# A gated output projection in a hybrid decoder block: the gate row in the weights, parked weights back by transfers, x on other queues

## The chip, the core and the metric

The kernel runs on one core of a Trainium2 chip. The metric is the device time of one execution in microseconds (us). The engines named below are PE (TensorE, matmuls), DVE (VectorE), ACT (ScalarE), POOL (GpSimd) and SP (SyncE, which here only issues transfers). Each engine works through its own list of instructions in order, and waits on semaphores for the others; a transfer (DMA) is issued by SP or ACT from that same list, so whatever waits in front of it holds it back.

## The reference, cut to what matters

Everything is float32; the sequence has 1024 rows and the model 1024 columns, the FFN 2816.

```python
mod = silu(c) @ w_ada + b_ada
sh1, sc1, g1, sh2, sc2, g2 = split(mod, 6)
h = rms_norm(x, norm_mix_g) * (1 + sc1) + sh1
proj = h @ w_in + b_in
...
y = (g_conv * y_conv + g_mlstm * y_mlstm) @ w_out
x = x + g1 * y
h = rms_norm(x, norm_ffn_g) * (1 + sc2) + sh2
gt, up = split(h @ w_ffn_up, 2)
x = x + g2 * ((silu(gt) * up) @ w_ffn_down)
return rms_norm(x, final_norm_g)
```

`g1` and `g2` are rows of 1024 values, the same for all rows of the sequence.

## The kernel before

Matmuls are done in three products per block: each float32 operand is split into a high part (a copy by ACT) and a low part (a subtraction by DVE), and PE adds high x high, low x high and high x low.

The stretch that the change touches lies in the middle of the kernel:

- **The end of the merge.** For eight column blocks `e`, PE multiplies the convolution's output by `w_conv_pw` (L158). DVE adds the bias and the gate (L926), adds the other mixer's part (L927), ACT writes the high part of `y` (L930), DVE the low part (L931). In the background DVE builds the four rows `g1`, `sh2`, `sc2`, `g2` of `mod` from 32 pieces of `w_ada` (`awt`, L900), PE transposes the sums (L904), and the result stands as columns in `modc`.
- **The gate rows.** After the last of these, PE transposes the columns of `g1` and `g2` (L939), ACT copies them (L940), SP stores them to a small array in HBM (`mrow_d`, L942). SP then loads the row of `g1`, repeated over 128 partitions, into `g1row` (L945); the row of `g2` is loaded later.
- **The output projection**, `w_out_part`: two halves `q` of the sequence times two halves `eh` of the columns, so four parts. Each has four chunks `kk` of `w_out`, 512 KB each: SP loads one into one of two buffers `wraw` (L996), ACT writes `whi` (L997), DVE writes `wlo` (L998), two buffers each. PE does 24 matmuls of 128 x 512 per chunk (L1003 to L1005) into four banks. At a part's end DVE multiplies each bank by `g1row` (L1009) and adds it to `x` (L1010), and ACT squares it for the norm (L1011). After the second `eh`, SP stores the new rows (`x1_d`, L1013) and they are scaled by their norm (L1016, L1018).
- **Beside it**: ACT issues the loads of `x` (L986). Two blocks of up weights (`f` = 0 and 1) are loaded early (L1047), combined (L1060 to L1065), split and *parked* in those halves of the tiles `Th` and `Tl` that are still free (`up_park`); later `up_unpark` copies them on ACT into the tiles `u` and `s` (L1097), which take the place of `y`. `h2_parts` transposes the normalized rows (L1028) and builds the seven-product operands of the up projection (`Bh`, `Th`, `Dh` and their low parts), which starts right after the projection (`up_run`, L1114 to L1116).

A scheduler sets the order on each engine from the order of the code and its priorities; `queue_behind` pins one instruction behind another on the same engine, and the table `AT` says at which of the 68 steps of the projection a task of the side work is put in. Tiles of a pool share space with tiles of earlier pools, and a load into one waits until the old tile's readers are done.

Of the kernel before, what the change touches and what calls it, by code (L numbers as in the profile page):

```python
# [8 lines left out]
F32 = mybir.dt.float32  # L9
# [8 lines left out]
KT = 8  # L18
NH = 4
FF = 2816  # L20
# [28 lines left out]
def hybrid_block(ctx: ExitStack, tc: tile.TileContext, x, c, w_ada, b_ada, norm_mix_g, w_in, b_in,  # L49
# [832 lines left out]

    modc = const.tile([128, 4, KT], F32, name="modc")

    def ada_task(ch, half):
# [24 lines left out]
        for k2 in range(4):  # L910
            bg.append((1300, lambda k2=k2: step(k2)))
# [19 lines left out]
            nc.vector.tensor_sub(y_lo, sg[:, q * 512:(q + 1) * 512], y_hi.bitcast(F32))  # L931
    pump(10 ** 9)
    credit[0] = 0.0
    g1, sh2, sc2, g2 = (modc[:, i, :] for i in range(4))
    mrow_d = [dram.tile([8, 128], F32, name=f"mrow_d{i}") for i in range(2)]
    p = ps_a()
    mrow = ap_.tile([8, 2, 128], F32, name="mrow", tag="act", bufs=3)
    for i, t in enumerate((g1, g2)):
        nc.tensor.transpose(p[0:8, i * 128:(i + 1) * 128], t, ident)  # L939
    nc.scalar.activation(mrow, p[0:8, 0:256].rearrange("p (i d) -> p i d", i=2), AF.Copy)  # L940
    for i in range(2):
        nc.sync.dma_start(mrow_d[i], mrow[:, i])  # L942

    def mod_row(i, t):
        nc.sync.dma_start(t, mrow_d[i].rearrange("(o k) d -> o (k d)", o=1).to_broadcast([128, D]))  # L945

# [21 lines left out]
    def krow(name):  # L968
        return up_.tile([128, D], F32, name=name, tag="krow", bufs=1)

    Bh = [big.tile([128, 2, 512], F32R, name=f"Bh{k}", tag="xa") for k in range(4)]
    Bl = [big.tile([128, 2, 512], F32R, name=f"Bl{k}", tag="xa") for k in range(4)]
    Th = [tp.tile([128, 4, 512], F32R, name=f"Th{k}") for k in range(4)]
# [7 lines left out]
        rsqrt(y, v)  # L981
        return y

    def load_x(t, xs):
        x = kx("x1")
        nc.scalar.dma_start(x, x2[t * 128:(t + 1) * 128, :])  # L986
        xs.append(x)

    evicted = {}

    def w_out_part(q, eh, xs, ss, banks):
        es = slice(eh * 512, (eh + 1) * 512)
        for kk in range(4):
            raw, hi, lo = (wp.tile([128, KT, 128], dt, name=n, tag=n).rearrange("p (k a) e -> p k (a e)", a=4)
                           for n, dt in (("wraw", F32), ("whi", F32R), ("wlo", F32R)))
            nc.sync.dma_start(raw, wo[kk * 256:(kk + 1) * 256, es].rearrange("(k p) e -> p k e", p=128))  # L996
            nc.scalar.activation(hi, raw, AF.Copy)  # L997
            nc.vector.tensor_sub(lo, raw, hi.bitcast(F32))  # L998
            y_hi, y_lo = (yt[q][j][kk] for j in range(2))
            for t in range(4):  # L1000
                ts_ = slice(t * 128, (t + 1) * 128)
                for k in range(2):
                    nc.tensor.matmul(banks[t], y_hi[:, k, ts_], hi[:, k, :], start=(kk == 0 and k == 0), stop=False)  # L1003
                    nc.tensor.matmul(banks[t], y_lo[:, k, ts_], hi[:, k, :], start=False, stop=False)
                    nc.tensor.matmul(banks[t], y_hi[:, k, ts_], lo[:, k, :], start=False, stop=(kk == 3 and k == 1))  # L1005
                yield
        for t in range(4):
            x = xs[t][:, es]
            nc.vector.tensor_mul(banks[t], banks[t], g1row[:, es])  # L1009
            evicted["v"] = nc.vector.tensor_add(x, x, banks[t])  # L1010
            evicted["s"] = nc.scalar.activation(banks[t], x, AF.Square, scale=1.0 / 32, accum_out=ss[:, t, eh:eh + 1])  # L1011
            if eh == 1:
                nc.sync.dma_start(x1_d[4 * q + t], xs[t])  # L1013
# [29 lines left out]
    def weights(kind, name):  # L1043
        return wp.tile([128, KT, 128], F32 if kind == "wraw" else F32R, name=name, tag=kind)

    def up_load(f, t, col0):
        nc.sync.dma_start(t, wup[:, col0 + f * 128:col0 + (f + 1) * 128].rearrange("(k p) e -> p k e", p=128))  # L1047
        return t

    def split_into(hi, lo, t):  # L1050
# [2 lines left out]
        return hi, lo  # L1053

    def up_sums(f, gate=True, behind=None):
        g = up_load(f, weights("wraw", "graw") if gate else k4("graw").rearrange("p (k e) -> p k e", k=KT), 0)
        u = up_load(f, k4("uraw").rearrange("p (k e) -> p k e", k=KT), FF)
# [32 lines left out]
    def up_unpark(f, s3):  # L1090
# [3 lines left out]
        for kp, name in ((3 - 2 * f, "u"), (2 - 2 * f, "s")):  # L1094
            pair = xb_pair(name)
            for t, src in zip(pair, spare(kp)):
                nc.scalar.activation(t.rearrange("p (a b) e -> p a (b e)", b=2), src.bitcast(F32), AF.Copy)  # L1097
            w.append(pair)
        return w + [s3]

# [79 lines left out]
        nc.vector.tensor_sub(lo, raw, hi.bitcast(F32))  # L1180
        return hi, lo

    xs0, xs1 = [], []
# [153 lines left out]
```

## Time and profile before

| what | value |
|---|---|
| three runs | 1732.58, 1734.45 (median), 1735.91 us |
| the profiled execution | 1735.88 us |
| its span, first to last instruction | 1734.1 us |
| granted clock of PE, mean over the span | 0.996 |

A row of a list of instructions has the start in us, the duration, the engine, the line, the operation and its tiles (out<-in), how many rows are merged, and in brackets how long the engine was idle before it and what ended that. "SPq" or "ACTq" in the engine's place are instructions that the engine only issues. A row of the waits says who waited for what: the total in us, how often, the longest. A row of windows has a stretch of the span, its length, the busy time of each engine with the number of instructions, the granted clock, the DMA engines' busy share and GB/s. A row of a line's summary has the number of instructions and the shortest, median and longest duration in ns.

### The profile page before, as it was taken

The numbers are of one execution on the slowest core, as the hardware profiler recorded it, in microseconds if no ns is written. First come the engines' busy times: TensorE is split into PE (matmuls) and PEld (weight loads), VectorE is DVE, ScalarE is ACT, GpSimd is POOL, SyncE is SP. The second block draws the span as 40 slices with busy tenths as digits, with TensorE's granted clock in tenths as the row PEclk, the third lists the DMA queues.
The fourth block names the chain that finished last, engine by engine and source line by source line (L and its number), as shares of the span: only waits on it lengthen the run. The fifth ranks groups of instructions, "written<-read, shape, count | busy, mean of one in ns | idle before, by whom it ended". The sixth has DMA issues, their size and how long they took to land. (4 is left out here: it accounts for less than half of the span.)

```text
span 1734.1 us, 20875 instructions
## 1 busy us (share of the span) xinstructions
PE 1692.9 (98%) x8360; PEld 1418.6 (82%) x8360; DVE 1249.7 (72%) x1681; ACT 611.7 (35%) x809; POOL 52.7 (3%) x113
## 2 busy tenths in 40 slices
PE   5999999999999999999999998999999999999998
PEld 4788889888988888888888778888888888778887
DVE  6989998997799669446798668766666665685243
ACT  7424335323433253223522386322222222232122
POOL 0000001000001000000000000000000000000000
PEclk9999999999999999999999999999999999999999
DMA  9221120221111112243694743322222222653121
GB/s 320 63 62 49 37 71 28 61 73 49 37 49 61 61 49 61 73 146 98 209 376 167 230 152 104 98 86 85 86 73 75 84 81 96 226 168 101 58 94 52
DMA packets 194711, 179.91 MB, mean 104 GB/s; under 512 B 7463, under 2 KB 166711, under 8 KB 194615
## 3 DMA queue, kind: packets, MB, share of 16 engines
q1 hardware_dynamic: 177367, 146.61, 27.4%
q10 hardware_dynamic: 17248, 31.99, 5.0%
q8 instruction: 65, 1.06, 0.3%
q14 instruction: 31, 0.25, 0.0%
HBM read 146.06 MB, written 32.51 MB: 103 GB/s over the span
## 5 line engine op out<-in xcount | busy, mean ns | idle before, releaser
L388 DVE SCALAR_TENSOR_TENSOR cacc<-a,col,cacc 128x1024 f32<-128x1024 f32 x240 | 306.8, 1286 | 3.9 <-ACT cacc L386 1.4
L158 PE MATMUL mm<-hh,wlo 128*128 128x512 f32 x864 | 271.2, 391 | 1.5 <-DVE wlo L149 1.5
L158 PE MATMUL mm<-hl,whi 128*128 128x512 f32 x864 | 272.5, 392 | 0.0
L158 PE MATMUL mm<-hh,whi 128*128 128x512 f32 x864 | 271.6, 392 | 0.0
L158 PEld LDWEIGHTS mm<-hh,wlo 128*128 128x128 f32 x864 | 160.3, 188 | 33.6 <-DVE wlo L149 2.7
L158 PEld LDWEIGHTS mm<-hl,whi 128*128 128x128 f32 x864 | 161.0, 188 | 32.1 <-issue 0.5
L158 PEld LDWEIGHTS mm<-hh,whi 128*128 128x128 f32 x864 | 160.5, 188 | 31.6
L148 ACT ACTIVATE whi<-wraw 128x1024 fp32r<-128x1024 f32 x61 | 64.7, 1061 | 226.5 <-PE mm L158 171.3
L149 DVE TENSOR_TENSOR wlo<-wraw,whi 128x1024 fp32r<-128x1024 f32 x61 | 74.5, 1222 | 28.7 <-ACT whi L148 25.2
L1114 PE MATMUL mm<-Bh,gh 128*128 128x512 f32 (+1 forms) x192 | 71.5, 375 | 2.9 <-ACT gh L1051 1.5
L1115 PE MATMUL mm<-Bl,gh 128*128 128x512 f32 (+1 forms) x192 | 71.5, 373 | 0.6 <-DVE Bl L1033 0.6
L604 PE MATMUL mm<-wlo,hh 128*128 128x256 f32 x256 | 72.0, 282 | 0.0
L1116 PE MATMUL mm<-Bh,gl 128*128 128x512 f32 (+1 forms) x192 | 71.2, 371 | 0.0
L1303 DVE TENSOR_TENSOR x<-x,mm 128x1024 f32<-128x1024 f32 x24 | 29.3, 1219 | 52.0 <-PE mm L1301 49.6
L1179 ACT ACTIVATE whi<-wraw 128x512 fp32r<-128x512 f32 (+2 forms) x32 | 25.3, 792 | 114.8 <-PE mm L1301 75.8
L535 DVE SCALAR_TENSOR_TENSOR cacc<-qkraw,col,cacc 128x1024 f32<-128x1024 f32 x48 | 61.5, 1282 | 4.9 <-ACT cacc L533 4.5
L603 PE MATMUL mm<-whi,hh 128*128 128x256 f32 x192 | 54.6, 284 | 0.0
L605 PE MATMUL mm<-whi,hl 128*128 128x256 f32 x192 | 54.2, 283 | 0.0
L1299 PE MATMUL mm<-fa,whi 128*128 128x512 f32 x128 | 50.6, 396 | 1.6 <-DVE cu L1142 0.9
L1300 PE MATMUL mm<-fa,wlo 128*128 128x512 f32 x128 | 50.5, 395 | 1.2 <-DVE wlo L1180 1.2
L1301 PE MATMUL mm<-fa,whi 128*128 128x512 f32 x128 | 50.6, 395 | 0.0
L1052 DVE TENSOR_TENSOR ul<-uraw,uh 128x1024 fp32r<-128x1024 f32 x20 | 24.5, 1225 | 35.4 <-ACT uh L1051 35.4
(444 smaller groups left out, 3893.1 us busy)
## 6 DMA issues: line engine op xcount, KB each, us to landing
wraw<-in_w_in_dram SPq DMA_DIRECT2D x64, 512.0 KB
awt<-in_w_ada_dram SPq DMA_DIRECT2D x32, 512.0 KB
graw<-in_w_ffn_up_dram SPq DMA_DIRECT2D x24, 512.0 KB
uraw<-in_w_ffn_up_dram SPq DMA_DIRECT2D x22, 512.0 KB
draw<-in_w_ffn_down_dram SPq DMA_DIRECT2D x22, 512.0 KB
act_d<-cg ACTq DMA_DIRECT2D x38, 256.0 KB
wad<-in_w_ada_dram SPq DMA_DIRECT2D x16, 512.0 KB
wraw<-in_w_out_dram SPq DMA_DIRECT2D x16, 512.0 KB
```

Source lines behind the costliest of these rows:

```text
L148: nc.scalar.activation(hi, raw, AF.Copy)
L149: (eng or nc.vector).tensor_sub(lo, raw, hi.bitcast(F32))
L158: nc.tensor.matmul(flat(acc)[:, a:b], lhs[:, k, :], rhs[k][:, a:b], start=(first and k == 0), stop=(last and k == kt - 1))
L388: nc.vector.scalar_tensor_tensor(acc, a[:, j:j + S], dw_col(j, ct), acc, op0=OP.mult, op1=OP.add)
L535: nc.vector.scalar_tensor_tensor(cv, raw[:, j:j + S], wcol(j), cv, op0=OP.mult, op1=OP.add)
L603: nc.tensor.matmul(o, hh[k][:, ts_], his[k], start=False, stop=False)
L604: nc.tensor.matmul(o[:, 0:256], hh[k][:, ts_], los[k], start=False, stop=False)
L605: nc.tensor.matmul(o, hl[k][:, ts_], his[k], start=False, stop=(k == KT - 1))
L1114: nc.tensor.matmul(o, a, rh, start=(k == 0), stop=False)
L1115: nc.tensor.matmul(o, a, rl, start=False, stop=False)
L1116: nc.tensor.matmul(o, b, rh, start=False, stop=(k == 3))
L1299: nc.tensor.matmul(o, hi[:, i, :], his[i][:, a:b], start=(i == 0), stop=False)
```

## The change

Four things are changed.

1. The row of `g1` is stored as soon as its columns are done (`store_row`, inside the background task of `mod`), the row of `g2` likewise at the end; the load of `g1row` is issued ahead of the projection, and so are the loads of the first `x` rows.
2. In `w_out_part`, each loaded chunk of `w_out` is multiplied by the row (L1006) before it is split; the multiply of each bank at a part's end is gone. What is computed is `y @ (w_out * g1)`.
3. `up_unpark` moves the parked blocks by eight transfers on SP's queue (L1108) in the place of eight copies on ACT.
4. The stores of `x1_d` are issued by ACT (L1022) in the place of SP; the two parked blocks' loads are pinned behind the last w_out load issued so far.

```diff
+    def store_row(ch):
+        p = ps_a()
+        mrow = ap_.tile([8, 128], F32, name="mrow", tag="mrow", bufs=1)
+        nc.tensor.transpose(p[0:8, 0:128], modc[:, ch, :], ident)
+        nc.scalar.activation(mrow, p[0:8, 0:128], AF.Copy)
+        nc.sync.dma_start(mrow_d[ch // 3], mrow)
...
+                if half and ch in (0, 3):
+                    store_row(ch)
...
-    p = ps_a()
-    mrow = ap_.tile([8, 2, 128], F32, name="mrow", tag="act", bufs=3)
-    for i, t in enumerate((g1, g2)):
-        nc.tensor.transpose(p[0:8, i * 128:(i + 1) * 128], t, ident)
-    nc.scalar.activation(mrow, p[0:8, 0:256].rearrange("p (i d) -> p i d", i=2), AF.Copy)
-    for i in range(2):
-        nc.sync.dma_start(mrow_d[i], mrow[:, i])
...
+    g1row = krow("g1row")
+    mod_row(0, g1row)
...
+    for t in range(4):
+        load_x(t, xs0)
...
-            nc.sync.dma_start(raw, wo[kk * 256:(kk + 1) * 256, es].rearrange("(k p) e -> p k e", p=128))
+            evicted["q"] = nc.sync.dma_start(raw, wo[kk * 256:(kk + 1) * 256, es].rearrange("(k p) e -> p k e", p=128))
+            nc.vector.tensor_mul(raw, raw, g1row[:, None, es].to_broadcast([128, 2, 512]))
...
-            nc.vector.tensor_mul(banks[t], banks[t], g1row[:, es])
             evicted["v"] = nc.vector.tensor_add(x, x, banks[t])
...
-                nc.sync.dma_start(x1_d[4 * q + t], xs[t])
+                nc.scalar.dma_start(x1_d[4 * q + t], xs[t])
...
-    def up_load(f, t, col0):
-        nc.sync.dma_start(t, wup[:, col0 + f * 128:col0 + (f + 1) * 128].rearrange("(k p) e -> p k e", p=128))
+    def up_load(f, t, col0, behind=None):
+        ins = nc.sync.dma_start(t, wup[:, col0 + f * 128:col0 + (f + 1) * 128].rearrange("(k p) e -> p k e", p=128))
+        if behind:
+            queue_behind(ins, behind["q"])
         return t
...
-                nc.scalar.activation(t.rearrange("p (a b) e -> p a (b e)", b=2), src.bitcast(F32), AF.Copy)
+                nc.sync.dma_start(t.rearrange("p (a b) e -> p a (b e)", b=2).bitcast(F32), src.bitcast(F32))
...
-    g1row = krow("g1row")
-    mod_row(0, g1row)
...
-    for t in range(4):
-        load_x(t, xs0)
```

The change moves instructions on three engines. First DVE, where the merge ends and the projection begins. Numbers tell buffers apart; the last two blocks of the merge are `t4b_7392` and `t4b_7481` before and the last is `t4b_7493` in the change; the first chunk of w_out is `wraw_7621` before and `wraw_7624` in the change. Before, around the last two blocks:

```order
L926 SCALAR_TENSOR_TENSOR t4b_7392<-mm_7402,col2_528,t4b_7392 128x1024
L998 TENSOR_TENSOR wlo_7623<-wraw_7621,whi_7622 128x1024
L900 SCALAR_TENSOR_TENSOR aacc_7451<-awt_7464,sc_c_102,aacc_7451 128x512
L906 TENSOR_REDUCE modc_6817<-pa_7379 128x4
L927 TENSOR_TENSOR t4b_7392<-t4b_7392,t4b_7393 128x1024
```
```order
L926 SCALAR_TENSOR_TENSOR t4b_7481<-mm_7491,col2_528,t4b_7481 128x1024
L998 TENSOR_TENSOR wlo_7653<-wraw_7651,whi_7652 128x1024
L908 TENSOR_TENSOR modc_6817<-modc_6817,col6_117 128x4
L927 TENSOR_TENSOR t4b_7481<-t4b_7481,t4b_7482 128x1024
L931 TENSOR_TENSOR y013_6825<-t4b_7481,y003_6821 128x512
L931 TENSOR_TENSOR y113_6833<-t4b_7481,y103_6829 128x512
L998 TENSOR_TENSOR wlo_7683<-wraw_7681,whi_7682 128x1024
```

And in the change (L937, L938 and L942 are the former L926, L927 and L931; L1006 is the new multiply, L1008 the former L998):

```order
L937 SCALAR_TENSOR_TENSOR t4b_7493<-mm_7503,col2_528,t4b_7493 128x1024
L938 TENSOR_TENSOR t4b_7493<-t4b_7493,t4b_7494 128x1024
L942 TENSOR_TENSOR y013_6827<-t4b_7493,y003_6823 128x512
L942 TENSOR_TENSOR y113_6835<-t4b_7493,y103_6831 128x512
L1006 TENSOR_TENSOR wraw_7624<-wraw_7624,g1row_7577 128x1024
L1006 TENSOR_TENSOR wraw_7655<-wraw_7655,g1row_7577 128x1024
L1008 TENSOR_TENSOR wlo_7626<-wraw_7624,whi_7625 128x1024
L1008 TENSOR_TENSOR wlo_7657<-wraw_7655,whi_7656 128x1024
L1006 TENSOR_TENSOR wraw_7686<-wraw_7686,g1row_7577 128x1024
L1006 TENSOR_TENSOR wraw_7717<-wraw_7717,g1row_7577 128x1024
L1008 TENSOR_TENSOR wlo_7688<-wraw_7686,whi_7687 128x1024
L1006 TENSOR_TENSOR wraw_7756<-wraw_7756,g1row_7577 128x1024
```

The first two low parts of w_out stood among the work of the last two merge blocks; now the first scaling stands behind all of it, and from the third chunk on a scaling stands ahead of the low part of the chunk before it.

Second SP at the same place, where `mrow_d1` is the stored row of g2 and `graw`, `uraw` are the first parked block's loads. Before:

```order
L996 DMA wraw_7711<-in_w_out_dram 128x2x512
L942 DMA mrow_d0_7546<-mrow_7549 8x128
L942 DMA mrow_d1_7547<-mrow_7549 8x128
L996 DMA wraw_7753<-in_w_out_dram 128x2x512
L945 DMA g1row_7600<-mrow_d0_7546 128x1024
L1047 DMA graw_7765<-in_w_ffn_up_dram 128x8x128
```

And in the change:

```order
L1005 DMA wraw_7655<-in_w_out_dram 128x2x512
L892 DMA mrow_d1_6819<-mrow_7483 8x128
L947 DMA g1row_7577<-mrow_d0_6818 128x1024
L1005 DMA wraw_7686<-in_w_out_dram 128x2x512
L1005 DMA wraw_7717<-in_w_out_dram 128x2x512
L1005 DMA wraw_7756<-in_w_out_dram 128x2x512
L1056 DMA graw_7769<-in_w_ffn_up_dram 128x8x128
```

The row of g1 goes to HBM many rows earlier (it isn't in this piece any more), but its load stands behind the store of the row of g2, and ahead of the third chunk instead of behind the fifth.

Third SP at the end of the projection in the change, where the eight new transfers stand among the loads of up weights:

```order
L1005 DMA wraw_8267<-in_w_out_dram 128x2x512
L1108 DMA uh_8292<-Th1_7596 128x4x256
L1108 DMA ul_8293<-Tl1_7600 128x4x256
L1056 DMA graw_8286<-in_w_ffn_up_dram 128x8x128
L1108 DMA sh_8296<-Th0_7595 128x4x256
L1108 DMA sl_8297<-Tl0_7599 128x4x256
L1056 DMA graw_8312<-in_w_ffn_up_dram 128x8x128
L1108 DMA uh_8318<-Th3_7598 128x4x256
L1108 DMA ul_8319<-Tl3_7602 128x4x256
L1056 DMA graw_8866<-in_w_ffn_up_dram 128x8x128
L1108 DMA sh_8322<-Th2_7597 128x4x256
L1108 DMA sl_8323<-Tl2_7601 128x4x256
```

They were copies on ACT (L1097); each pair now waits on SP until PE has read the tiles of `y` whose place it takes, which is at the end of chunks 13, 14, 15 and 16.

More of the change, by code (lines that the diff above doesn't have):

```diff
@@ L883, in hybrid_block @@
     modc = const.tile([128, 4, KT], F32, name="modc")
+    mrow_d = [dram.tile([8, 128], F32, name=f"mrow_d{i}") for i in range(2)]
+    def store_row(ch):
[4 more added lines that the diff above has]
+        nc.sync.dma_start(mrow_d[ch // 3], mrow)
     def ada_task(ch, half):
@@ L933, in hybrid_block @@
     credit[0] = 0.0
-    g1, sh2, sc2, g2 = (modc[:, i, :] for i in range(4))
-    mrow_d = [dram.tile([8, 128], F32, name=f"mrow_d{i}") for i in range(2)]
-    p = ps_a()
-    mrow = ap_.tile([8, 2, 128], F32, name="mrow", tag="act", bufs=3)
-    for i, t in enumerate((g1, g2)):
-        nc.tensor.transpose(p[0:8, i * 128:(i + 1) * 128], t, ident)
-    nc.scalar.activation(mrow, p[0:8, 0:256].rearrange("p (i d) -> p i d", i=2), AF.Copy)
-    for i in range(2):
-        nc.sync.dma_start(mrow_d[i], mrow[:, i])
+    sh2, sc2 = (modc[:, i, :] for i in range(1, 3))
     def mod_row(i, t):
@@ L969, in krow, with load_x @@
         return up_.tile([128, D], F32, name=name, tag="krow", bufs=1)
+    g1row = krow("g1row")
+    mod_row(0, g1row)
+    def load_x(t, xs):
+        x = kx("x1")
+        nc.scalar.dma_start(x, x2[t * 128:(t + 1) * 128, :])
+        xs.append(x)
+    xs0, xs1 = [], []
+    for t in range(4):
+        load_x(t, xs0)
     Bh = [big.tile([128, 2, 512], F32R, name=f"Bh{k}", tag="xa") for k in range(4)]
@@ L982, in rsqrt_mean @@
         return y
[L984 to L987, printed above, removed]
     evicted = {}
@@ L1055, in up_sums @@
     def up_sums(f, gate=True, behind=None):
-        g = up_load(f, weights("wraw", "graw") if gate else k4("graw").rearrange("p (k e) -> p k e", k=KT), 0)
-        u = up_load(f, k4("uraw").rearrange("p (k e) -> p k e", k=KT), FF)
+        g = up_load(f, weights("wraw", "graw") if gate else k4("graw").rearrange("p (k e) -> p k e", k=KT), 0, behind)
+        u = up_load(f, k4("uraw").rearrange("p (k e) -> p k e", k=KT), FF, behind)
         gw = split_into(weights("whi", "gh"), weights("wlo", "gl"), g) if gate else None
@@ L1181, in act_split @@
         return hi, lo
-    xs0, xs1 = [], []
     ss0, ss1 = (up_.tile([128, 4, 4], F32, name=f"ss{i}") for i in range(2))
-    g1row = krow("g1row")
-    mod_row(0, g1row)
     def banks(n):
```

## The prediction

> **What bounds the kernel now.** I read the page's totals first, then the stretch that the change touches as windows, then what TensorE waited for in it.
>
> ```profile
> span 1734.1 us, 20875 instructions
> PE 1692.9 (98%) x8360; PEld 1418.6 (82%) x8360; DVE 1249.7 (72%) x1681; ACT 611.7 (35%) x809; POOL 52.7 (3%) x113
> ```
>
> TensorE (PE) is busy for 1692.9 of 1734.1 us, so no edit can gain more than its 41 us of waits, and every new wait of PE counts in full. The page's profiled run took 1735.88 us, 1.78 us more than its span; the median of the runs shown is 1734.45. I work out a difference against the profiled run and add it to the median.
>
> ```profile
> core 0: us, PE busy (x) PEld busy (x) DVE busy (x) ACT busy (x) POOL busy (x), PEclk, DMA share, GB/s
> 945.30:972.90 27.60, 27.60 (x123) 22.36 (x121) 15.00 (x20) 7.91 (x15) 0.00 (x0) 1.00 0.74 239
> 972.90:1002.30 29.40, 26.85 (x118) 21.81 (x118) 22.40 (x31) 15.62 (x22) 2.95 (x4) 1.00 0.54 172
> 1002.30:1039.70 37.40, 37.40 (x181) 30.77 (x179) 25.42 (x42) 29.19 (x42) 0.10 (x1) 1.00 0.43 141
> 1039.70:1049.30 9.60, 6.35 (x50) 5.81 (x49) 8.11 (x15) 6.24 (x15) 1.90 (x3) 1.00 0.80 261
> 1049.30:1100.00 50.70, 48.26 (x356) 44.81 (x357) 42.60 (x85) 27.66 (x43) 0.55 (x1) 1.00 0.29 91
> ```
>
> The output projection runs from 945.3 to 1039.7; then comes the hand-off to the up projection, then the second half of h2 up to 1100. PE is idle 2.55 us in the second row, 3.25 in the fourth and 2.44 in the fifth. Together 8.2 us: that is all that can be won here.
>
> ```profile
> PE pa L1003 <- ACT whi L997: 1.5, 1, 1.5
> PE mm L1114 <- ACT gh L1051: 1.5, 1, 1.5
> PE mm L1114 <- ACT mm L1011: 1.3, 1, 1.3
> PE mm L1005 <- DVE wlo L998: 1.0, 1, 1.0
> ...
> PE pc L1114 <- ACT sh L1097: 0.4, 1, 0.4
> ```
>
> The waits of PE in this stretch: 1.5 and 1.0 within the projection, for a chunk's high and low parts; 1.5, 1.3 and 0.4 at the hand-off.
>
> **The change, part by part.** I number the 16 chunks of w_out (four per part) in the order in which PE uses them. Two starts of PE with eleven steps between them:
>
> ```profile
> 960.13 0.39 PE L1004 MATMUL mm<-whi,y 128*128 128x512 f32 x1
> ...
> 962.62 0.39 PE L1004 MATMUL mm<-whi,y 128*128 128x512 f32 x1
> ```
>
> That is a matmul every 0.227 us, and 5.45 us for the 24 of a chunk.
>
> *1. The first chunk waits for the scaling.* Before, it was split while the merge still ran. Now, in DVE's order, its scaling stands behind the last merge subtraction, and that comes from PE's last merge matmul.
>
> ```profile
> 944.75 0.71 PE L158 MATMUL mm<-ah,wlo 128*128 128x512 f32 x2
> 945.30 0.39 PE L1003 MATMUL mm<-whi,y 128*128 128x512 f32 x1
> ```
> ```profile
> 945.64 1.28 DVE L926 SCALAR_TENSOR_TENSOR t4b<-mm,col,t4b 128x1024 f32<-128x1024 f32 x1
> 946.83 1.22 DVE L998 TENSOR_TENSOR wlo<-wraw,whi 128x1024 fp32r<-128x1024 f32 x1
> ...
> 948.03 1.22 DVE L927 TENSOR_TENSOR t4b<-t4b 128x1024 f32<-128x1024 f32 x1
> 949.96 1.29 DVE L931 TENSOR_TENSOR y<-t4b,y 128x512 fp32r<-128x512 f32 x2 [0.70 <-ACT y L930]
> ```
> ```profile
> 949.29 1.15 ACT L930 ACTIVATE y<-t4b 128x512 fp32r<-128x512 f32 x2 [3.59 <-DVE t4b L927]
> 951.38 1.06 ACT L997 ACTIVATE whi<-wraw 128x1024 fp32r<-128x1024 f32 x1 [0.94 <-ACT y L930]
> ```
>
> PE now moves from the merge to the projection without a gap. In the new order the merge's tail is the same without the split between: 945.5 + 1.2 (L926) + 1.2 (L927) = 947.9, the first subtraction 0.67 after ScalarE starts, two of them 1.25: 949.8. Only then may the first scaling start, and it also needs the gate row. That row's transfer stands on SP behind the store of the second row, which waits for a transpose that PE now does right after its last merge matmul.
>
> ```profile
> 952.49 0.27 PE L939 MATMUL pa<-ident,modc 128*8 128x128 f32 x1
> ```
> ```profile
> 948.08 0.37 SPq L996 DMA_DIRECT2D wraw<-in_w_out_dram  x1
> 953.20 0.64 SPq L942 DMA_DIRECT2D mrow_d<-mrow  x2
> ...
> 956.41 0.35 SPq L945 DMA_DIRECT2D g1row<-mrow_d  x1
> ```
> ```profile
> 950.00:951.00 1.00, 1.00 (x6) 0.83 (x5) 1.00 (x2) 0.44 (x1) 0.00 (x0) 1.00 0.83 313
> 951.00:952.00 1.00, 1.00 (x6) 0.84 (x5) 0.25 (x1) 0.62 (x1) 0.00 (x0) 1.00 0.14 53
> ...
> 958.00:959.00 1.00, 1.00 (x7) 0.81 (x6) 0.00 (x0) 1.00 (x1) 0.00 (x0) 1.00 0.92 184
> ...
> 965.00:966.00 1.00, 1.00 (x6) 0.83 (x5) 0.69 (x1) 0.00 (x0) 0.00 (x0) 1.00 1.03 388
> ```
> ```profile
> SPq L996 <- DMA g1row<-mrow_d: 5.3, 1, 5.3
> ```
>
> From that transpose to SP's first store are 0.71 us: store at 946.0, the row's transfer one place later, 946.35. How long does it take? A lone 512 KB load, issued at 948.08, moved its last bytes just after 951 and needs some 3.3 us with its signal: 949.65. Among the x loads the same row took until about 963.7 (SP's wait), 7.3 us: 953.65. The lone load is the nearer row, as nothing else is in flight at 946. But while this row moved (958) the engines were 92% busy at only 184 GB/s, so I add 0.8: 950.45.
>
> ```profile
> L1162 DVE TENSOR_TENSOR draw<-draw,g2row x22: 1218/1226/1227, 1467.6 to 1579.5; 128x1024 f32<-128x1024 f32 x22
> ```
>
> The down projection's own scaling has the new scaling's shape and takes 1.22 us (1.13 to the next instruction). So: scaled 951.65, ScalarE's copy of 1.06 (L997) 952.75, against PE free at 945.5: **7.25 us**. The low part needs the second scaling and the subtraction, 954.0, and PE has four matmuls before it (0.9): 0.35 more. Term **+7.6**, between 6.8 (the row is there in time) and 10.8.
>
> *2. The split becomes a ring.* DVE's order puts the scaling of chunk n+2 ahead of the low part of chunk n+1, and that load goes into the buffer that the low part of n frees. So one step is load + scaling + subtraction: 3.3 + 1.13 + 1.13 + 0.1 = 5.65 us, against PE's 5.45. Loads 3 and 4 start at 954.0 and 955.2 among six x loads; eight times 0.52 MB from 950.4 on at the 388 GB/s of the stretch at 965, shared by turns, lands load 4 near 960.5 and the third low part at 962.85. Six steps on, the ninth is at 996.75, and at about 999.2 with the two pairs of parked up blocks that pass through the same queue and the same DVE. PE wants it at 945.5 + 7.6 + 8 x 5.45 + 0.9 = 997.6: 1.6 late. The tenth stands behind four evictions and two subtractions of the park (some 4.7): about 1007, against 1004.65: 2.4. Together **+4.0**; bounds 0 (a step no longer than PE's) and 11 (a load one us longer in each of seven steps). Before, the same stretch held 1.5 + 1.0, which belong to the old order: **-2.5**. Behind chunk 10 the third row above has slack on all engines, and I add nothing.
>
> *3. Evictions without the multiply.*
>
> ```profile
> 993.14 0.69 DVE L1009 TENSOR_TENSOR pn<-pn,g1row 128x512 f32<-128x512 f32 x1
> 993.74 0.69 DVE L1009 TENSOR_TENSOR pc<-pc,g1row 128x512 f32<-128x512 f32 x1
> ```
>
> Sixteen of these go, 0.60 apart, 9.6 us; the 16 scalings add 18.1, so DVE has 8.5 us more to do. What counts is the hand-off, where DVE's evictions hold PE's banks: four multiplies (2.4) go there, and the scalings are over. What is late next is the low part of the gate block, which now stands just behind the third eviction (0.9 of waiting), and the last eviction's square (0.3): 1.2 instead of 3.25, **-2.0**; bounds 0 and -3.25.
>
> *4. Parked blocks by transfers.*
>
> ```profile
> L1097 ACT ACTIVATE sh<-Th x2: 1043/1044/1044, 1029.9 to 1041.2; 128x1024 fp32r<-128x1024 f32 x2
> ```
>
> Eight such copies, 8.3 us, leave ScalarE, which is not the bound; the 0.4 wait for one is in term 3. The last pair of transfers may start only when PE has read the buffers, at the end of the projection, and is needed after five products of 12 matmuls and the 1.2 us of waits, some 7 us later. No transfer within SBUF is in the trace. By the lone load a pair lands in 3.3 + 1.5 = 4.8 us: cost 0. By the rate of 184 it takes 3.3 + 2.9 and stands behind earlier pairs that also lag: +3.5. I take 0, as the lone load is the nearer row. A page alone has a price: by "DMA: Bandwidth & Descriptors" (Trainium skill), section "Anatomy of one DMA", an estimate for 512 KB is 2.0 + 1.2 us, which would leave the sum as it is.
>
> *5. Queues.* Loads of x were on ScalarE's queue already and move only in order; stores of x1 leave SP.
>
> ```profile
> L1013 SPq DMA_DIRECT2D x_d<-x x8: 319/337/344, 995.0 to 1048.4; - x8
> ```
>
> Eight issues of 0.34 us on an engine busy 35% of the time: 0, hidden beside PE.
>
> Sum: 7.6 + 4.0 - 2.5 - 2.0 = **+7.1**: 1743.0 against the profiled run, 1741.6 against the median.
>
> **The clock.**
>
> ```profile
> 30.80:37.50 6.70, 6.62 (x18) 5.19 (x18) 6.42 (x9) 3.42 (x4) 0.00 (x0) 0.54 1.09 348
> ```
> ```profile
> 30.88 6.74 PE L308 MATMUL mm<-hh,wf 128*128 128x512 f32 x16 [2.12 <-ACT hh L297]
> ```
>
> After a sparse start and a wait of 2.12 us PE ran at a granted clock of 0.54, and 16 matmuls took 6.74 us instead of 16 x 0.227 + 0.16 = 3.8. The 7.25 us of idleness in term 1 are longer than any wait since, so a loss of up to 2.9 us is likely there. If the ring is the limit, as in term 2, it costs nothing: a later PE waits 2.9 us less in chunks 9 and 10. The Trainium skill, "TensorE: Matmul & The Clock Gate", section "What's actually happening", says that about 3.4 us of idleness halve the clock and about 3.4 us of sustained work restore it, by which the sum would be 1.7 higher; the slow stretch measured above is longer than that.
>
> **Rivals.**
> - *The clock's loss adds on top*, because the ring is itself paced by PE (ScalarE's copy waits until PE has left a high part's buffer): 7.1 + 2.9, **1744.5**. For: those buffers are two. Against: the ring's slowest part is the load.
> - *Loads are slower than alone*, one us each over seven steps: term 2 is 11: 1734.45 + 14.1 = **1748.6**. For: the fourth row above shows 261 GB/s, and more transfers come. Against: around chunks 5 to 10 the engines are half idle (0.54).
> - *The parked blocks come late*: +3.5, **1745.1**. For: 512 KB in short pieces, and graw loads between. Against: the 7 us of cover.
> - *The hand-off pays it back, and the kernel is not slower.* The row is in time and the ring keeps up (6.8 - 2.5), the hand-off's waits go whole (-3.25), and the lighter DVE queue takes up to the 2.44 behind it: +1.05 to -1.35, **1733.1 to 1735.5**. It decides once the start costs no more than 5.75 + 2.44 = 8.2. For: the start's bound is below that. Against: all four at once are needed, the clock included.
>
> **How the numbers follow.** Forecast 1741.6: 0.45. Clock on top 0.17, slow loads 0.13, late blocks 0.11, paid back 0.14. The range 1736.5 to 1749.5 leaves out most of the last and the far end of the slow loads. A difference below 0.2% (3.5 us: 1731.0 to 1737.9) is about what a measurement here can't tell from none. Same 0.12, the paid-back case but for the 0.02 that I leave to faster, which needs more than all that I see to win; slower 0.86, the other four.
>
> **What would show it.** Term 1: a PE wait of about 7 us before its first projection matmul, ended by the high part's copy, that copy by the first scaling, and that by the row or the last merge subtraction; a clock below 1.00 just behind it. Term 2: low parts some 5.7 us apart, and PE waits of 1.5 to 2.5 us at chunks 9 and 10. Term 3: at most 1.5 us of waits at the hand-off. Term 4: no PE wait ended by a transfer within SBUF. I am wrong if the first projection matmul starts before 950, or if PE waits more than 12 us in the ring.

## The result and the profile after

| | before | changed |
|---|---|---|
| median | 1734.56 us (4 runs, 1732.58 to 1735.91) | 1749.33 us (4 runs, 1748.12 to 1751.10) |
| profiled execution | 1735.88 us, span 1734.1 | 1749.13 us, span 1747.4 |
| mean granted clock | 0.996 | 0.992 |

The ratio is 1.0087, with a 95% interval of 1.0074 to 1.0100: 14.8 us slower. The forecast was 7.1 us slower, half of it; 1749.33 lies at the very end of the range given (1749.5).

The page's totals of the changed kernel, whose span is 1747.4 us:

```profile
PE 1699.3 (97%) x8360; PEld 1424.0 (81%) x8360; DVE 1258.5 (72%) x1681; ACT 602.5 (34%) x802; POOL 52.6 (3%) x113
```

The span is 13.3 us longer, but PE is also busy 6.4 us longer with the same 8360 matmuls. So about half of the loss is waiting and half looks like slower matmuls. PE's waits in the stretch of the change (who waited <- for what: total us, times, longest):

```profile
PE mm L1013 <- ACT whi L1007: 8.0, 2, 7.5
PE mm L1015 <- DVE wlo L1008: 3.2, 2, 1.8
PE mm L1125 <- ACT gh L1062: 1.9, 1, 1.9
...
PE pa L1015 <- DVE wlo L1008: 0.6, 1, 0.6
...
PE mm L1127 <- DVE gl L1063: 0.5, 1, 0.5
...
PE pa L1125 <- DMA sh<-Th: 0.4, 1, 0.4
```

The first is the gap ahead of the projection (7.5, and 0.5 at the ninth chunk); L1015 and the rest of L1013 are waits in the ring, 4.4 us together; L1125 and L1127 are the hand-off, 2.8. The stages as windows; behind the engines' busy times stand the granted clock, the DMA share and GB/s:

```profile
944.54:952.04 7.50, 0.00 (x1) 0.00 (x0) 6.05 (x7) 2.52 (x5) 0.00 (x0) 0.69 0.65 215
952.04:958.17 6.13, 6.13 (x15) 4.85 (x16) 2.34 (x2) 0.90 (x1) 0.00 (x0) 0.54 0.99 380
...
985.00:1012.00 27.00, 22.63 (x96) 17.41 (x95) 22.64 (x29) 11.84 (x19) 1.81 (x2) 1.00 0.59 194
...
1053.10:1060.00 6.90, 6.35 (x28) 6.06 (x29) 3.85 (x7) 2.96 (x7) 1.08 (x2) 0.51 1.08 387
```

Behind both long waits of PE the clock is about half: 6.13 us for 15 matmuls at the start (15 x 0.227 = 3.4, so 2.7 lost), and 6.9 us at the hand-off. The forecast had the first and not the second.

To place the loss, I cut both spans at the same four points, each the first or last start of a line of matmuls. "Gap" is from the last merge matmul to the first of the projection, "projection" from there to its last, "up" from there to the last matmul of the up projection (hand-off included), "rest" what follows.

| | merge ends | gap | projection | up | rest | span |
|---|---|---|---|---|---|---|
| before | 944.75 | 0.55 | 94.1 | 441.0 | 253.7 | 1734.1 |
| changed | 943.80 | 8.24 | 98.8 | 442.6 | 254.0 | 1747.4 |
| difference | -0.95 | +7.69 | +4.7 | +1.6 | +0.3 | +13.3 |
| forecast | 0 | +7.6 | +1.5 | -2.0 | 0 | +7.1 |

The gap is as forecast (0.35 of the 7.6 was for the first low part, which falls into the projection column). The projection lost some 3 us more than forecast, and the up stage, which begins with the hand-off, lost 1.6 where 2.0 were to be gained. The first and last columns differ from run to run without an edit to them: over all profiled executions below the merge ends between 943.7 and 945.3, and the rest takes 251.7 to 254.3. The last section shows that the first of them goes with a half clock early in the kernel.

### The profile page after: what moved, and what is told of

The parts are those of the page before. It is cut to its first block, busy times and chain, and to the rows that moved or that the text cites. A ratio compares the mean times of both kernels' runs of the same rounds, so it can differ in the third digit from the quotient of the medians.

```text
span 1747.4 us, 20886 instructions
## 1 busy us (share of the span) xinstructions
PE 1699.3 (97%) x8360; PEld 1424.0 (81%) x8360; DVE 1258.5 (72%) x1681; ACT 602.5 (34%) x802; POOL 52.6 (3%) x113
## 4 chain that ended last, share of the span: by engine, by line
PE 85%; DVE 7%; DMA 4%; issue 2%; ACT 1%; POOL 0%; ACTq 0%; SPq 0%; POOLq 0%; DVEq 0%
PE mm L158 39%; PE mm L1125 4%; PE mm L1126 4%; PE mm L1127 4%; PE mm L1306 2%; PE mm L1305 2%; PE mm L1307 2%; PE mm L603 1%; PE mm L605 1%; PE mm L604 1%; DMA wraw<-in_w_out_dram 1%; PE pc L1125 1%; PE pc L1127 1%; PE pc L1126 1%; DVE macc L277 1%
## 5 line engine op out<-in xcount | busy, mean ns | idle before, releaser
L148 ACT ACTIVATE whi<-wraw 128x1024 fp32r<-128x1024 f32 x61 | 64.7, 1060 | 229.1 <-PE mm L158 172.9
L1125 PE MATMUL mm<-Bh,gh 128*128 128x512 f32 (+1 forms) x192 | 72.4, 380 | 1.9 <-ACT gh L1062 1.9
L1127 PE MATMUL mm<-Bh,gl 128*128 128x512 f32 (+1 forms) x192 | 72.4, 378 | 0.5 <-DVE gl L1063 0.5
```

The costliest lines, as they stand in the source:

```text
L1125: nc.tensor.matmul(o, a, rh, start=(k == 0), stop=False)
L1127: nc.tensor.matmul(o, b, rh, start=False, stop=(k == 3))
```

## The experiments

The theory to test: the two steps that failed are the ring's pace and the transfers of the parked blocks, and the half clock behind the gap costs nothing beside them. The rivals: the clock's loss comes on top; the hand-off is held by evictions; the queues cost something. The table has the median of each kernel, its ratio to the kernel before in the same group of runs, and the stages of its profiled execution.

| run | median us | ratio (95%) | gap | projection | up |
|---|---|---|---|---|---|
| e1_late_multiply | 1735.95 | 1.0012 (1.0003 to 1.0022) | 0.45 | 92.1 | 443.7 |
| e2_warm_start | 1749.81 | 1.0094 (1.0079 to 1.0109) | 8.29 | 98.9 | 442.0 |
| e3_order | 1744.27 | 1.0063 (1.0048 to 1.0078) | 8.62 | 93.9 | 443.6 |
| e4_first_part | 1739.70 | 1.0031 (1.0020 to 1.0042) | 0.45 | 97.3 | 444.3 |
| e5_act_unpark | 1746.62 | 1.0072 (1.0060 to 1.0085) | 7.89 | 100.0 | 440.0 |
| e6_order_act | 1739.92 | 1.0037 (1.0023 to 1.0051) | 8.09 | 92.7 | 439.3 |
| e7_first_order_act | 1731.62 | 0.9992 (0.9983 to 1.0000) | 0.46 | 94.6 | 439.1 |
| e8_rows_queues | 1732.89 | 0.9998 (0.9989 to 1.0007) | 0.46 | 92.8 | 441.3 |
| e9_order_pool | 1756.49 | 1.0133 (1.0118 to 1.0147) | 7.67 | 94.0 | 456.5 |
| e10_ahead | 1729.90 | 0.9975 (0.9964 to 0.9985) | 0.46 | 92.2 | 438.8 |
| e11_last_part | 1734.48 | 1.0003 (0.9994 to 1.0012) | 0.46 | 97.1 | 440.7 |

The kernel before took 1734.1 (beside e1 to e4), 1733.4 (e5 to e8) and 1734.4 (e9 to e11).

### e1_late_multiply: the fold undone

```diff
-            nc.vector.tensor_mul(raw, raw, g1row[:, None, es].to_broadcast([128, 2, 512]))
...
+            nc.vector.tensor_mul(banks[t], banks[t], g1row[:, es])
             evicted["v"] = nc.vector.tensor_add(x, x, banks[t])
```

> The fold alone is undone: the banks are multiplied at a part's end again; the early rows, the transfers of the parked blocks and the queues stay as in the change. Theory A (the fold makes the whole loss, the rest costs nothing): 1734.6, within 1.5 us, no half clock behind the merge and none at the hand-off. Rival B (transfers and queues make the hand-off's part of the loss, waits of 2.8 us and 3.1 us of half clock): 1737 to 1740.

1735.95, ratio 1.0012: gap and ring are gone, so the fold makes nearly all of the loss. But the hand-off is worse than before by 2.7 us (443.7 against 441.0). Its longest wait of PE at the hand-off, and the window around it:

```profile
1041.31 0.58 PE L1125 MATMUL mm<-Bh,gh 128*128 128x256 f32 x1 [3.52 <-ACT gh L1062]
```
```profile
1041.00:1048.00 7.00, 5.44 (x24) 4.89 (x25) 5.05 (x11) 4.62 (x11) 2.10 (x4) 0.54 1.05 365
```

With 0.99 more for the block's low part at 1043.08, PE waits 4.5 us there, with the DMA engines full (1.05) and the clock at about half (0.54). A gain of 2 us inside the projection (92.1 against 94.1) covers most of it. So B holds for the hand-off, though the time alone looked like A.

### e2_warm_start: the clock kept up in the gap

```diff
+    warm = ps_n()
+    for i in range(30):
+        ins = nc.tensor.matmul(warm, yt[0][0][0][:, 0, 0:128], yt[0][0][0][:, 0, :], start=True, stop=True)
+        queue_behind(ins, last[0])
+        last[0] = ins
```

> The change with 30 more matmuls whose result is not used, in the 7.5 us in which TensorE waits for the first high part. Theory A (the ring of load, scaling and subtraction sets the pace, so the 2.8 us that the half clock took at the start are hidden under it): the clock is 1.00 at the start, the waits in the ring grow from 4.4 to about 7.2 us, the time stays at 1749. Rival B (the clock's loss adds on top): the waits in the ring stay at 4.4 and the time falls by 2.8, to 1746.5.

The order of instructions on DVE, SP and POOL is that of the change. Windows of this run: the first half of the ring, its second half, and the hand-off:

```profile
953.19:985.00 31.81, 31.00 (x133) 24.67 (x134) 16.05 (x16) 7.48 (x12) 0.00 (x0) 1.00 0.54 182
985.00:1012.50 27.50, 22.45 (x94) 16.96 (x93) 23.39 (x31) 12.71 (x21) 1.06 (x1) 1.00 0.58 191
...
1052.46:1063.70 11.24, 6.76 (x49) 5.95 (x49) 5.47 (x11) 5.05 (x11) 2.17 (x4) 1.00 1.08 380
```

The clock is 1.00 from the first matmul, PE is through its first chunks sooner, and waits for it: idle 0.81 + 5.05 = 5.9 us in the ring instead of 4.4 (A had named 7.2). The projection takes 98.9 us, as in the change (98.8), and the time is 1749.8. So A holds in the time: the half clock at the start costs nothing, because the ring ends later than PE anyway. This execution had no half clock at the hand-off either, though no edit was made there, and its up stage was only 0.6 shorter (442.0): PE's waits there are 3.4 us (1.68, 0.76 and 0.93) instead of 2.8.

### e3_order: the low part ahead of the next scaling

```diff
+            mul = nc.vector.tensor_mul(raw, raw, g1row[:, None, es].to_broadcast([128, 2, 512]))
+            low.append(mul)
+            if len(low) >= 3:
+                queue_behind(mul, low[-2])
...
+            low[-1] = nc.vector.tensor_sub(lo, raw, hi.bitcast(F32))
```

> The change with another order on VectorE: from the third chunk on a chunk's scaling stands behind the low part of the chunk before it, not ahead of it. Theory A (the ring is VectorE's order: the low part n+1 waits for load n+2): the 4.4 us of waits in the ring go, 1745. Rival B (the loads or ScalarE's copies set that pace in any order): the waits stay, 1749.

1744.27: A. The projection falls from 98.8 to 93.9 us, less than before's 94.1, and in the ring only 0.6 us of waiting is left. So the ring was the order on DVE. Its pace in the changed kernel is read from SP's and DVE's rows, load n+2 issued behind low part n and the scaling waiting for it:

```profile
970.39 0.37 SPq L1005 DMA_DIRECT2D wraw<-in_w_out_dram  x1
...
976.66 0.37 SPq L1005 DMA_DIRECT2D wraw<-in_w_out_dram  x1
```
```profile
974.27 1.23 DVE L1006 TENSOR_TENSOR wraw<-wraw,g1row 128x1024 f32<-128x1024 f32 x1 [3.91 <-DMA wraw<-in_w_out_dram]
975.41 1.22 DVE L1008 TENSOR_TENSOR wlo<-wraw,whi 128x1024 fp32r<-128x1024 f32 x1
...
980.53 1.23 DVE L1006 TENSOR_TENSOR wraw<-wraw,g1row 128x1024 f32<-128x1024 f32 x1 [1.23 <-DMA wraw<-in_w_out_dram]
981.67 1.22 DVE L1008 TENSOR_TENSOR wlo<-wraw,whi 128x1024 fp32r<-128x1024 f32 x1
```

From the issue to the scaling are 3.88 and 3.87 us, with hardly another transfer in flight, and a step is 981.67 - 975.41 = 6.26. What the faster projection uncovers is the hand-off:

```profile
PE pa L1129 <- DMA sh<-Th: 2.8, 1, 2.8
```

PE now waits 2.8 us for a parked block's transfer (0.4 in the change), beside 1.2 and 0.9 for the gate block's two parts.

### e4_first_part: the first part not folded

```diff
-            nc.vector.tensor_mul(raw, raw, g1row[:, None, es].to_broadcast([128, 2, 512]))
+            if (q, eh) != (0, 0):
+                nc.vector.tensor_mul(raw, raw, g1row[:, None, es].to_broadcast([128, 2, 512]))
...
+            if (q, eh) == (0, 0):
+                nc.vector.tensor_mul(banks[t], banks[t], g1row[:, es])
```

> The change with the first of the four parts left as before: its four chunks are not scaled, its banks are multiplied at its end. Theory A (start of the ring and its pace make the loss up to the hand-off): the wait of 7.5 us and its 2.8 us of half clock go, and the ring starts four chunks later with loads ahead of it, so that 0 to 4.4 us of its waits go too: 1734.6 to 1739. Rival B (the first scaled part, or the multiplied first banks, bring the same wait one part later): 1743 or more.

1739.70, 0.7 above A's range: the gap is gone (0.45), and PE waits 1.9 us at the sixth chunk in its place. Part of what was won comes back at the hand-off, where PE waits 5.1 us for a gate block's high part (up 444.3).

### e5_act_unpark, e6_order_act, e8_rows_queues: the transfers undone

All three have the copies of ScalarE back, e5 in the change, e6 with e3's order, e8 with e1's late multiply:

```diff
-                nc.sync.dma_start(t.rearrange("p (a b) e -> p a (b e)", b=2).bitcast(F32), src.bitcast(F32))
+                nc.scalar.activation(t.rearrange("p (a b) e -> p a (b e)", b=2), src.bitcast(F32), AF.Copy)
```

> The change with the parked blocks copied by ScalarE again; fold, early rows and queues stay. Theory A (the eight transfers fill the DMA engines and SP's queue at the hand-off, so that the gate blocks and the last parked pair come late): the hand-off's 2.8 us of waits fall to about 1.5 and its 3.1 us of half clock go, 1745 to 1747. Rival B (VectorE's evictions and ScalarE's squares hold the hand-off, and the copies add to ScalarE's work there): 1749 to 1751.

> The order of e3_order and the copies by ScalarE together. e3_order took 1744.3 and has 4.95 us of waits at its hand-off, 2.8 of them for a transfer of a parked block. Theory A (transfers): those 2.8 and some of the rest go, 1740 to 1742, so that what is left above the kernel before is the start. Rival B (ScalarE has no room for eight copies at the hand-off): 1743.5 or more.

> Only the early rows, the early loads of x and the stores on ScalarE's queue: fold and transfers are both undone. Theory A (queues cost nothing): 1734.4, within 0.8 us, and e1_late_multiply's 1.9 us over the kernel before are the transfers'. Rival B (stores behind ScalarE's work, rows ahead on SP): 1736, the same as e1_late_multiply.

All three came out as A: e5 within its range, e6 0.1 us below, and e8 0.5 below the kernel before of its own group. With against without transfers, the up stage takes 442.6 against 440.0 (the change and e5), 443.6 against 439.3 (e3 and e6), 443.7 against 441.3 (e1 and e8): the transfers cost 2.4 to 4.3 us, and the ratios of the whole kernels in the table differ by as much. Part of that can go through the half clock, which comes at the hand-off in some executions; but in e2, which had none, the stage is still 2.0 longer than in e5. e5's ring waits stay (projection 100.0, against 98.8 in the change), as nothing there was changed. And e8, which keeps only the early rows and the queues, is at 0.9998: these cost nothing. What the transfers add is seen in the same stretch, 1025 to 1062, of e3_order and then e6_order_act (DMA packets, MB moved, mean rate):

```profile
DMA packets 9523, 10.00 MB, mean 270 GB/s; under 512 B 304, under 2 KB 8496, under 8 KB 9520
```
```profile
DMA packets 5303, 5.81 MB, mean 157 GB/s; under 512 B 176, under 2 KB 4277, under 8 KB 5301
```

Eight transfers are 4.19 MB more, through engines that the last x loads, the stores of x1 and the gate blocks already use. In e3_order the block for which PE waited was issued as follows, and PE got it 11.4 us later:

```profile
1046.50 0.60 SPq L1112 DMA_DIRECT2D sh<-Th  x1
```
```profile
1057.93 0.38 PE L1129 MATMUL pa<-Th,sh 128*128 128x256 f32 x1 [2.81 <-DMA sh<-Th]
```

The projection's last matmul, which reads the tile that this block goes into, started at 1046.3, so the transfer could hardly have been issued sooner. What held it was its way through the engines, and there the two hardware queues are worth comparing while PE waits. This is e3_order between 1052 and 1056, first ACT's queue, which stores x1, then SP's, which moves the parked and the gate blocks (packets, MB, share of the engines' time):

```profile
q10 hardware_dynamic: 351, 1.30, 79.6%
q1 hardware_dynamic: 358, 0.34, 24.3%
```

The queues get equally many packets through, but a store's is some 3.7 KB and one of SP's queue 0.95 KB. So the blocks for which PE waits get a fifth of the bytes. In the changed kernel it is the same (1055 to 1060: 466 packets with 1.71 MB against 459 with 0.33 MB). This points at the fourth part of the change, the stores on ACT's queue, as a partner of the third; as no run has the transfers with the stores on SP's queue, it isn't shown.

### e9_order_pool: the transfers on another queue

```diff
-                nc.sync.dma_start(t.rearrange("p (a b) e -> p a (b e)", b=2).bitcast(F32), src.bitcast(F32))
+                nc.gpsimd.dma_start(t.rearrange("p (a b) e -> p a (b e)", b=2).bitcast(F32), src.bitcast(F32))
```

> e3_order with the eight transfers of the parked blocks issued by GpSimd, which is idle there, and not by SyncE; SyncE is left with the loads of the gate blocks. e3_order took 1744.3, the copies by ScalarE in its place 1739.9. Theory A (the transfers cost by what they move: the DMA engines are full around the hand-off): 1743 to 1746, and waits for the parked pair stay. Rival B (they cost by their place on SyncE, where each waits for a free tile with the gate loads behind it): 1739.5 to 1741.5.

Neither: 1756.49. On POOL's queue the transfers were issued 3.6 to 8.2 us apart, each about 0.3 us after the one before it had landed, and PE waited for two of them; behind these waits the granted clock was 0.50 from 1050 to 1070, which is a part of the loss. Two of POOL's rows, then PE's waits:

```profile
1049.78 0.76 POOL L1112 DMA_DIRECT2D uh<-Th  x1 [5.05 <-issue]
1057.95 0.76 POOL L1112 DMA_DIRECT2D ul<-Tl  x1 [7.42 <-issue]
```

```profile
PE mm L1129 <- DMA uh<-Th: 3.2, 1, 3.2
PE mm L1131 <- DMA ul<-Tl: 2.8, 1, 2.8
```

This queue has a pace of its own, so the run does not tell volume from SP's order. How the 2.4 to 4.3 us divide between the added bytes, the stores beside them and gate loads that stand behind waiting transfers on SP stays open.

### e7_first_order_act, e10_ahead and e11_last_part: a better version

e7 joins e4's first part, the order of e3 and the copies. In e10 the second scaled chunk is loaded and scaled ahead of the first part's evictions as well:

```diff
+        if (q, eh) == (0, 0):
+            w_split(0, 1, 0)
+            scaled(0, 1, 1)
         for t in range(4):
             x = xs[t][:, es]
```

(`scaled` issues a chunk's load and its scaling behind the last low part, `w_split` splits it; a chunk done ahead is not done again.)

> First part unscaled as in e4_first_part, scaling behind the earlier low part from the second part on, parked blocks copied by ScalarE. e4_first_part took 1739.7 with 5.6 us of waits and some 3 us of half clock at its hand-off, and 2.3 us at its first scaled chunk. Theory A: hand-off as before or better, 1732 to 1735, no slower than the kernel before. Rival B (the scalings' 12 x 1.13 us hold VectorE, and with it the hand-off): 1737 or more.

> e7_first_order_act (1731.6), with the second scaled chunk's load and scaling put ahead of the first part's evictions on VectorE. There TensorE waits 1.96 us for that chunk, since its scaling stands behind 9 instructions of the eviction, and then runs 12 matmuls at 0.43 in the place of 0.23 us. Theory A: wait and half clock go, 1727 to 1729, faster than both kernels. Rival B (that chunk's load is late itself, among the loads of x and of the up blocks): 1731 to 1733.

e7 took 1731.62, which can't be told from the kernel before. Its wait for the second scaled chunk, and the window behind it:

```profile
973.70 0.50 PE L1015 MATMUL pa<-whi,y 128*128 128x512 f32 x1 [1.96 <-ACT whi L1009]
```
```profile
973.70:978.20 4.50, 4.50 (x13) 3.55 (x14) 4.50 (x6) 2.37 (x3) 0.00 (x0) 0.62 0.29 87
```

And of e10, the same:

```profile
973.11 0.50 PE L1031 MATMUL pa<-whi,y 128*128 128x512 f32 x1 [1.12 <-ACT whi L1018]
```
```profile
973.10:980.00 6.90, 6.89 (x30) 5.70 (x31) 6.90 (x10) 3.83 (x7) 0.00 (x0) 1.00 0.29 77
```

1.12 us of the wait remain, the half clock is gone, and the projection falls from 94.6 to 92.2. Why a part of the wait stays is in DVE's rows of e10, an eviction's addition and the scaling straight behind it:

```profile
970.09 0.68 DVE L1042 TENSOR_TENSOR x<-x,mm 128x512 f32<-128x512 f32 x1
970.69 1.22 DVE L1011 TENSOR_TENSOR wraw<-wraw,g1row 128x1024 f32<-128x1024 f32 x1
```

The scaling waits for DVE and not for its load, which SP issued at 961.03. The code puts it ahead of the first part's evictions; on the chip it stands behind five of their instructions, where in e7 it stood behind nine. So A's cause holds, the edit did half of it, and the time lies between the two ranges. e10 takes 1729.90 us, 0.9975 (0.9964 to 0.9985) of the kernel before: faster than both kernels, 4.5 us than the one, 19 than the other.

In e11 only the last of the four parts is folded:

```diff
-            nc.vector.tensor_mul(raw, raw, g1row[:, None, es].to_broadcast([128, 2, 512]))
+            if (q, eh) == (1, 1):
+                ins = nc.vector.tensor_mul(raw, raw, g1row[:, None, es].to_broadcast([128, 2, 512]))
+                queue_behind(ins, evicted["low"])
...
+            if (q, eh) != (1, 1):
+                nc.vector.tensor_mul(banks[t], banks[t], g1row[:, es])
```

> The fold for the last of the four parts alone; the other three multiply their banks at their ends; scaling behind the earlier low part, parked blocks copied by ScalarE. e8_rows_queues, without any fold, took 1732.9 with 3.7 us of waits at the hand-off, e7_first_order_act 1.4 us there. Theory A (what the fold gains is only the shorter eviction at the hand-off, and it needs only the last part for it): 1730.5 to 1731.5. Rival B (four scalings late in the projection hold the low parts or the operands of the up projection): 1733 or more.

1734.48, B's time, by a way that B had only in part. A wait for a bank inside the projection appears, with a lower clock behind it (0.78 between 1022.4 and 1030). The bank's square on ACT waits for DVE's addition, and ahead of that eviction DVE, busy without a break, does a scaling of the last part:

```profile
1017.50 1.22 DVE L1007 TENSOR_TENSOR wraw<-wraw,g1row 128x1024 f32<-128x1024 f32 x1
```
```profile
1021.69 0.60 ACT L1024 ACTIVATE mm<-x 128x512 f32<-128x512 f32 x1 [2.15 <-DVE x L1023]
```
```profile
1022.47 0.50 PE L1015 MATMUL mm<-whi,y 128*128 128x512 f32 x1 [1.82 <-ACT mm L1024]
```

So the late scalings stand in the way, as B said, but what waits is an eviction's bank and not a chunk. At the hand-off the square's wait of 1.3 us is gone, as A said, and waits of 0.5 and 1.1 us for DVE come in its place (up 440.7).

## Why the prediction was half of the loss

**Term 1, the first chunk waits (+7.6): right in size, by luck in its parts.** The gap grew by 7.69. The chain of waits of the changed kernel shows what set it:

```profile
945.26 3.66 DMA g1row<-mrow_d
948.92 0.32 ACTq L978
...
949.77 1.12 ACTq L978
950.93 1.06 ACT whi L1007
```

The row was there at 948.92, in time for the end of the merge's last subtraction, so that counted from the merge's end the scaling started 0.55 us sooner than forecast. But ACT, whose issues of the x loads now stand ahead of the first copy, was not free until 950.89, some 0.8 us after the first scaling. The two errors cancel by luck: PE waits 7.5 us where I had 7.25. Term 5, which set the queues at 0, overlooked these issues; e8 shows that without the fold they indeed cost nothing.

**Term 2, the ring (+4.0, with -2.5 for the old waits): right mechanism, a term too small.** The step that failed is the price of a load. I took 3.3 us, read from a window one us wide in which it was still moving 53 GB/s. Measured: 3.9 from issue to use, and a step of 6.2 to 6.3 instead of 5.65 where nothing else is in DVE's way. The six steps from the third low part to the ninth took 38.8 us (962.47 to 1001.29) where I had 33.9, and 2.45 more for the parked blocks; these added only some 1 us, so that error hides a part of the other. The third low part itself was 0.85 late. DVE thus finished the ninth at 1002.5, not at 999.2. PE paid for it with 4.4 us of waits in the ring and the 2.7 of the half clock, 7.1 where I had 4.0. e3 shows that it is the ring: in another order on DVE the projection is 4.9 us shorter.

**The clock: right that it is hidden.** A half clock did come at the start and cost 2.7 us of PE's time, but e2 without it takes as long. The second half clock, at the hand-off, was not forecast; there e2, which had none, is 0.6 shorter. So of the 6.4 us of additional busy time in the page's totals hardly any is a loss of its own: without it PE waits instead.

**Term 3, evictions without the multiply (-2.0): right, but hidden behind term 4.** PE's wait of 1.3 us at the hand-off for the last bank's square, which the kernel before has and e8, with the multiplies, too, is gone in e5, e6, e7 and e10. Without transfers all of PE's waits there are 1.4 to 2.0 us in these four, against 3.25 before and 3.7 in e8, and the up stage is shorter than before by 1.0 (e5), 1.7 (e6), 1.9 (e7) and 2.2 (e10).

**Term 4, the transfers (0, up to +3.5): wrong.** I priced the last pair by a lone load, 4.8 us against 7 us of cover. Measured: 11.4 us from issue to use for the first block of the pair in e3, with the stores of x1 and the gate blocks in the same engines. The step that failed is the choice of the lone load as the nearest row: the row of the hand-off itself, 261 GB/s at a share of 0.80, stood in the prediction, and in it there was little room. It cost 2.4 to 4.3 us. The sign that was named for it, no wait of PE ended by a transfer within SBUF, failed as well: 0.4 us in the change, 2.8 in e3. The estimate of 3.2 us from the Trainium skill ("DMA: Bandwidth & Descriptors", section "Anatomy of one DMA") that stands beside the term, which the page gives for transfers issued by GpSimd, is as far from the 11.4 as the lone load's.

So the forecast's 7.1 becomes 7.1 + 3.2 (ring) + 3.6 (transfers in the place of the hand-off's gain) = 13.9, against 13.3 between the spans and 14.8 between the medians. The rest of the 14.8 is open; the 1.5 by which medians and spans differ lies within the spread of either kernel's runs. Of the rivals, "loads are slower" and "parked blocks come late" both came true in part and at once, though the loads of the ring were slow by 0.6 us each, alone in flight, and not by one us among others; "the clock adds on top" and "the hand-off pays it back" did not.

## What to carry to other kernels

A factor that is moved from a result to its weights moves a wait as well: what was needed at the end of a stage is now needed ahead of its first matmul. Leave the first part in the old form (here worth 8 us of gap), and let the other parts take the new one. When a preparing step in place is put between a load and its consumers, look at the order in which one engine serves two buffers: a step of chunk n+2 ahead of the last step of chunk n+1 makes a ring of the load's whole latency. And a copy that is taken from an engine with room (ACT was busy 35% of the time) and made a transfer is paid for where transfers are already many; price it in the stretch in which it runs, and look at the packets of what runs beside it.

## What the runs showed of the hardware

**Half clock after short waits, by where they fall.** The clock fell to half behind waits of PE of 1.91 us (the change, hand-off) and 1.96 (e7), but not behind one of 1.79 at the end of the ring (the change, at 1010.1). A stretch that the change doesn't touch has a wait of 1.77 us in both kernels, with a half clock behind it in the one alone. In these profiles the granted clock changes only at points that lie multiples of 3.41 us apart. Two such steps of before, then of the changed kernel, where they lie 0.9 us earlier:

```profile
269.07:272.48 3.41, 1.33 (x10) 0.92 (x8) 3.41 (x6) 1.27 (x3) 0.10 (x1) 1.00 0.21 35
272.48:275.90 3.42, 3.42 (x16) 3.42 (x17) 1.82 (x6) 3.39 (x7) 0.00 (x0) 0.50 0.40 118
```
```profile
268.14:271.56 3.42, 2.17 (x17) 1.76 (x15) 3.42 (x4) 1.70 (x3) 0.00 (x0) 1.00 0.01 2
271.56:274.97 3.41, 2.53 (x19) 2.32 (x20) 2.41 (x7) 2.99 (x6) 0.10 (x1) 1.00 0.58 152
```

In before all of the idle time falls into one step, 2.08 us, and the next step runs at half clock; in the change it is divided, 1.25 and 0.88, and nothing happens. Over the 13 profiles, between 30 and 1720 us, a step at full clock with 1.82 us or more of idle PE was followed by half clock, and one with 1.77 or less was not, but for two late ones (1.58 in e1 at 1542, 1.60 in e6 at 1546). The wait at 1010.1 is cut in two by such a point at 1008.8. This is read from the traces; no run was made to test it. So a wait of about 1.8 us sometimes costs its own length and sometimes up to 1.7 us more for each step of half clock. The merge ends at 944.7 to 944.9 in the five profiles with a half clock at 272 (before, e1, e2, e6, e11) and at 943.7 to 944.0 in seven without it; e4 (945.3) has its half clock at 54. The Trainium skill, "TensorE: Matmul & The Clock Gate", section "What's actually happening", puts the fall behind about 3.4 us of idleness; the runs here show it at little more than half of that.

**Transfers on GpSimd's queue came one at a time.** In e9_order_pool POOL was idle for up to 7.4 us ahead of an issue, waiting for nothing that the profile shows; between 1055 and 1060 the DMA engines were only 57% busy.

**Equal packets, unequal bytes.** While PE waited in e3_order (1052 to 1056), the queues of ACT and SP got 351 and 358 packets through, with 1.30 and 0.34 MB. In these windows a queue's part of the bytes went by the size of its packets.
